# First loads on two queues and in smaller parts, constant matmuls ahead of the data, another accumulator and GpSimd for the convolution's matrices, in a kernel of two transformer blocks

## The chip, the cores and the metric

The kernel runs on one core of a Trainium2 chip. The metric is device microseconds of one execution. TensorE multiplies matrices into eight PSUM accumulators ("banks" of 128 x 512 f32 each), VectorE, ScalarE and GpSimd do elementwise work, and DMA transfers are issued from the queue of SyncE (SP) and, after the change, of ScalarE too.

## What is computed

Two blocks on 256 tokens of 1024 features, all in f32. The part that matters here is the start of the first block:

```python
def first_block(x, p, mix_pre_norm, w_in, conv_dw_w, conv_dw_b, ...):
    h = rmsnorm(x, mix_pre_norm[i])
    u = h @ w_in[i]                        # 1024 x 3072
    u_a, u_b = u[..., :512], u[..., 512:1024]
    hq, hk, hv, hg = ...                   # 512 columns each
    y_conv = conformer_conv(u_a, u_b, ...) # u_a * sigmoid(u_b), causal depthwise
                                           # convolution of width 31, layernorm, silu
    y_ret = retention_group(hq, hk, hv, hg)
    y = concatenate([y_conv, y_ret]) @ w_out[i]
    x = x + rmsnorm(y, mix_post_norm[i])
    ...                                    # FFN, gate; then the second block
```

The second block (differential attention, neighbourhood attention, two FFNs) isn't touched.

## The kernel before

Activations lie with features on the 128 partitions: eight tiles `h[k]` of 128 x 256 tokens. Every f32 matrix product is made of three products of halves: `weights` (lines 122 to 133) casts a loaded piece `raw` to a high half on ScalarE (line 129) and takes the low half on VectorE (line 130); `split_scaled` (lines 150 to 152) does the same for x, scaled by a column of `vec`; `mm3` (lines 163 to 170) issues high by high, high by low, low by high. Loaded pieces share four buffers (`raw`), the halves five each (`hi`, `lo`), activations a ring of 16 (`x`).

`w_in` comes in blocks of 256 output columns. Block 0 is computed piece by piece while x arrives (lines 313 to 327): four pieces of 512 columns, each followed by two tiles of x, all issued from SP, behind `vec` (all constant columns, among them the norm's weights and the convolution's taps, line 101). `in_products` (line 329) makes a further block from two loads of 512 KB. Its accumulator comes from the pool `pmm`, which has three; the pool `pss` has two, for the convolution and the scores, and `pst` two, for small products.

The norm's reciprocal isn't applied to x but to the products. Squares of x are summed beside the work (`Stat`, from line 196), two tiny products and a power on GpSimd (line 194) make the reciprocal `rx`, and `times_r` (line 338) multiplies a finished accumulator by it, which also frees the accumulator. Blocks 0 to 3 feed the convolution. Channel group 0 is done with 31 taps on VectorE (line 396), groups 1 to 3 as products on TensorE (line 387): 32 x 32 diagonal matrices `cw` are made from `vec` by VectorE (line 372, two instructions a group, six in all, pinned behind the last weight split by `conv_pin`), and shifted copies of the input by ScalarE and VectorE (line 381). Blocks 4 to 7 are queries and keys.

A scheduler orders each engine's instructions by the program's order and by simulated times in which they become ready, and hands out the buffers of a pool as they come free; on the chip each engine then works through its list in that order.

## Time and profile before

| | us |
|---|---|
| median of 3 runs | 1422.79 (1421.12 to 1423.82) |
| the profiled execution | 1420.28 |
| its span, first to last instruction | 1418.4 |
| TensorE busy in the span | 1376.9 (97%) |
| VectorE, ScalarE, GpSimd busy | 1060.8, 697.1, 64.8 |
| loaded from HBM | 237.10 MB |

Times in the rows below are microseconds from the start of the span; an engine's idle time before an instruction stands in square brackets with what ended it. A matmul's end is modelled, so the distance between starts tells its pace.

### The profile page before, as it was taken

Reading aid. Unit: us, or ns where it says so; the run is one execution under the profiler, and the core shown is the slowest. Engines: PE = TensorE matmul, PEld = TensorE weight load, DVE = VectorE, ACT = ScalarE, POOL = GpSimd, SP = SyncE. Lnnn points to the kernel's source line nnn. Section 1 sums busy time; section 2 is a strip of 40 time slices with the busy share of each in tenths; the row PEclk is TensorE's granted clock in tenths of the full one; section 3 lists DMA queues with packets and bytes.
Section 4 is the critical chain, followed back from the end, with each engine's and each line's share of the span. In section 5 each row is a group of like instructions: output and inputs, shape, how many; then the busy total and the mean of one; then the engine's idle time right before and its main releaser. Section 6 shows DMA issues by size and latency. Waiting matters only on the chain.

```text
span 1418.4 us, 25707 instructions
## 1 busy us (share of the span) xinstructions
PE 1376.9 (97%) x9907; PEld 1260.0 (89%) x9907; DVE 1060.8 (75%) x2174; ACT 697.1 (49%) x1314; POOL 64.8 (5%) x116
## 2 busy tenths in 40 slices
PE   7998999999998999999999999999999999999997
PEld 6898899999997898799888888888998788899997
DVE  7975889986576789977799999965765457777653
ACT  6655544454464777654422222223554446654442
POOL 0000000000000223220000000000000000000000
PEclk9999999999999999999999999999999999999999
DMA  8457598667463334324565776634632224365462
GB/s 302 133 163 267 179 316 278 214 212 228 125 205 122 105 120 125 107 87 145 167 212 194 217 236 222 207 124 128 199 127 72 80 89 136 123 196 184 146 184 92
DMA packets 77739, 239.83 MB, mean 169 GB/s; under 512 B 8752, under 2 KB 13104, under 8 KB 77488
## 3 DMA queue, kind: packets, MB, share of 16 engines
q1 hardware_dynamic: 77616, 238.18, 52.2%
q8 instruction: 78, 1.28, 0.4%
q14 instruction: 45, 0.37, 0.1%
HBM read 237.10 MB, written 1.05 MB: 168 GB/s over the span
## 4 chain that ended last, share of the span: by engine, by line
PE 79%; issue 14%; ACT 2%; DVE 2%; DMA 2%; POOL 1%; SPq 0%; POOLq 0%; DVEq 0%; ACTq 0%
PE mm L168 20%; PE mm L169 19%; PE mm L170 19%; PE mm L177 2%; PE mm L178 2%; PE mm L179 2%; PE s L757 1%; PE o L1095 1%; PE t L782 1%; PE s L169 1%; PE s L170 1%; PE s L168 1%; PE s L1055 1%; PE t L1085 1%; ACT hi L129 1%
## 5 line engine op out<-in xcount | busy, mean ns | idle before, releaser
L129 ACT CAST hi<-raw 128x1024 fp32r<-128x1024 f32 (+2 forms) x382 | 365.2, 958 | 520.0 <-PE mm L169 327.3
L130 DVE TENSOR_TENSOR lo<-raw,hi 128x1024 fp32r<-128x1024 f32 (+2 forms) x382 | 422.3, 1107 | 173.3 <-ACT hi L129 170.2
L168 PE MATMUL mm<-x,hi 128*128 128x256 f32 (+2 forms) x1584 | 491.8, 314 | 13.3 <-ACT x L151 8.0
L169 PE MATMUL mm<-x,hi 128*128 128x256 f32 (+2 forms) x1584 | 491.3, 311 | 1.6 <-DVE x L619 1.3
L170 PE MATMUL mm<-x,lo 128*128 128x256 f32 (+2 forms) x1584 | 490.8, 311 | 0.8 <-DVE lo L130 0.8
L168 PEld LDWEIGHTS mm<-x,hi 128*128 128x128 f32 x1584 | 303.0, 193 | 42.3 <-issue 14.5
L170 PEld LDWEIGHTS mm<-x,lo 128*128 128x128 f32 x1584 | 304.9, 193 | 18.4 <-issue 3.4
L169 PEld LDWEIGHTS mm<-x,hi 128*128 128x128 f32 x1584 | 304.7, 193 | 17.9 <-issue 1.7
L263 DVE SCALAR_TENSOR_TENSOR junk<-adaw,sb 128x512 f32<-128x512 f32 x320 | 219.9, 687 | 11.2 <-DMA adaw<-ada 6.6
L168 PE MATMUL mm<-o,hi 128*128 128x256 f32 (+1 forms) x340 | 100.9, 303 | 2.3 <-ACT o L147 2.1
L170 PE MATMUL mm<-o,lo 128*128 128x256 f32 (+1 forms) x340 | 101.7, 301 | 0.0
L169 PE MATMUL mm<-o,hi 128*128 128x256 f32 (+1 forms) x340 | 101.5, 300 | 0.0
L168 PE MATMUL s<-x,hi 128*128 128x258 f32 (+1 forms) x304 | 86.2, 284 | 0.0
L169 PE MATMUL s<-x,hi 128*128 128x258 f32 (+1 forms) x304 | 86.2, 284 | 0.0
L170 PE MATMUL s<-x,lo 128*128 128x258 f32 (+1 forms) x304 | 86.2, 283 | 0.0
L169 PE MATMUL mm<-q,hi 128*128 128x256 f32 (+1 forms) x265 | 80.9, 305 | 0.0
L170 PE MATMUL mm<-q,lo 128*128 128x256 f32 (+1 forms) x265 | 80.8, 305 | 0.0
L168 PE MATMUL mm<-q,hi 128*128 128x256 f32 (+1 forms) x265 | 80.8, 305 | 0.0
L168 PEld LDWEIGHTS mm<-o,hi 128*128 128x128 f32 x340 | 65.2, 195 | 5.9 <-ACT o L147 2.8
L177 PE MATMUL mm<-hi,x 128*128 128x256 f32 x240 | 70.1, 292 | 0.0
L194 POOL TENSOR_TENSOR rv<-rv,mhalf 128x2 f32<-128x2 f32 (+1 forms) x16 | 14.5, 907 | 1200.3 <-DVE rv L193 1200.3
L179 PE MATMUL mm<-hi,x 128*128 128x256 f32 x240 | 69.1, 288 | 0.0
(242 smaller groups left out, 2138.5 us busy)
## 6 DMA issues: line engine op xcount, KB each, us to landing
raw<-gu SPq DMA_DIRECT2D x88, 512.0 KB, 4.0
adaw<-ada SPq DMA_DIRECT2D x80, 512.0 KB, 4.5
raw<-wqkv SPq DMA_DIRECT2D x72, 512.0 KB, 4.1
raw<-ffn SPq DMA_DIRECT2D x44, 512.0 KB, 5.4
raw<-down SPq DMA_DIRECT2D x37, 384.0 KB, 3.2
raw<-down SPq DMA_DIRECT2D x37, 320.0 KB, 3.0
raw<-w_in SPq DMA_DIRECT2D x22, 512.0 KB, 5.3
o<-ada SPq DMA_DIRECT2D x32, 256.0 KB, 5.5
```

Of the source, the lines that this page charges most:

```text
L129: last_conv[:] = [act.copy(hi[:, :n], raw[:, :n]).ins, dve.tensor_tensor(lo[:, :n], raw[:, :n], f32(hi[:, :n]), op=ALU.subtract).ins]
L130: dve.tensor_tensor(lo[:, :n], raw[:, :n], f32(hi[:, :n]), op=ALU.subtract).ins]
L168: pe.matmul(out, wh, xh, start=first and k == 0, stop=False)
L169: pe.matmul(out, wh, xl, start=False, stop=False)
L170: last_mm[0] = pe.matmul(out, wl, xh, start=False, stop=last and k == n - 1).ins
L177: pe.matmul(out, xh[:, ts_], wh, start=k == 0, stop=False)
L178: pe.matmul(out, xh[:, ts_], wl, start=False, stop=False)
L179: pe.matmul(out, xl[:, ts_], wh, start=False, stop=k == n - 1)
L194: pool.tensor_tensor(out, out, mhalf[:, :n], op=ALU.pow)
L263: dve.scalar_tensor_tensor(out=junk, in0=raw[:, gs_], scalar=1.0, in1=sb[:, v, gs_], op0=ALU.mult, op1=ALU.mult, accum_out=acc[:, n, v, g: ...
L757: mm = pe.matmul(ps[m], a_[ms, qs], b_[ms, k0:k0 + n], start=i == 0, stop=i == 2)
L782: mm = pe.matmul(po[:, :P], pT[:, j * P:(j + 1) * P], vv, start=j == 0, stop=j == nk - 1)
```

## The change

- `vec` is loaded in two parts. Its first eight columns (the weights of the first norm) are the first issue, from ScalarE's queue; the rest is issued from SP behind the loads of block 0.
- Eight f32 products of the constant tile `ones` with itself go into an accumulator of `pst` that nobody reads.
- Block 0's pieces: the first two of 256 columns, then three of 512. x0 and x1 are issued from ScalarE's queue, the others from SP.
- Block 3's accumulator comes from `pss`.
- The matrices `cw` are made on GpSimd, without the pin.

```diff
--- before.py
+++ after.py
@@
+WAKE = 8
@@
-    nc.sync.dma_start(out=vec, in_=a["vec"])
+
+    act.dma_start(out=vec[:, :8], in_=a["vec"][:, :8])
     ident = tab[:, C_ID:C_ID + P]
     ones = const.tile([P, P], F32, name="ones")
     dve.memset(ones, 1.0)
 
     first = small.tile([P, 1], F32, tag="first", name="first", bufs=1)
+
+    wake = bank(pst, "t")
+    for _ in range(WAKE):
+        pe.matmul(wake[:, :P], ones, ones, start=True, stop=True)
     act.activation(first, ones[:, 0:1], AF.Silu)
@@
-    for g in range(4):
-        raw = load(a["w_in"][0][:, g * 512:(g + 1) * 512], 512)
-        for k in (2 * g, 2 * g + 1):
-            nc.sync.dma_start(out=h[k], in_=a["x"][:, k, :])
-        (w,) = weights(None, (512,), [raw])
-        for k in (2 * g, 2 * g + 1):
+    for ks in ((0,), (1,), (2, 3), (4, 5), (6, 7)):
+        raw = load(a["w_in"][0][:, ks[0] * T:(ks[-1] + 1) * T], len(ks) * T)
+        for k in ks:
+            (act if k < 2 else nc.sync).dma_start(out=h[k], in_=a["x"][:, k, :])
+        (w,) = weights(None, (len(ks) * T,), [raw])
+        for k in ks:
@@
-                c0 = (k % 2) * T + j * P
+                c0 = (k - ks[0]) * T + j * P
@@
+    nc.sync.dma_start(out=vec[:, 8:], in_=a["vec"][:, 8:])
+
     def in_products(i):
         w = w_blocks(a["w_in"][i])
-        ps = bank(pmm, "mm")
+
+        ps = bank(pss, "s") if i == 3 else bank(pmm, "mm")
@@
-        conv_pin = last_conv[1]
@@
-            with tc.issue_after(conv_pin):
-                for i in range(nd // 16, 2):
-                    d0 = V_DWW + c * 32 + i * 16
-                    dve.tensor_tensor(
-                        cw[i].rearrange("p (n m) -> p n m", m=32), vec[:, V_MASK:V_MASK + 32].unsqueeze(1).to_broadcast([P, 16, 32]),
-                        vec[:, d0:d0 + 16].unsqueeze(2).to_broadcast([P, 16, 32]), op=ALU.mult)
+            for i in range(nd // 16, 2):
+                d0 = V_DWW + c * 32 + i * 16
+                pool.tensor_tensor(
+                    cw[i].rearrange("p (n m) -> p n m", m=32), vec[:, V_MASK:V_MASK + 32].unsqueeze(1).to_broadcast([P, 16, 32]),
+                    vec[:, d0:d0 + 16].unsqueeze(2).to_broadcast([P, 16, 32]), op=ALU.mult)
```

## Rows read from the trace of the kernel before

**Rows 1.** The page: span, and busy time of each engine with its share.

```profile
span 1418.4 us, 25707 instructions
PE 1376.9 (97%) x9907; PEld 1260.0 (89%) x9907; DVE 1060.8 (75%) x2174; ACT 697.1 (49%) x1314; POOL 64.8 (5%) x116
```

**Rows 2.** Waits of TensorE, 0 to 62 us: total, times, longest.

```profile
PE mm L168 <- ACT x L151: 6.2, 1, 6.2
PE mm L168 <- DVE t L338: 2.4, 1, 2.4
```

**Rows 3.** Stretches: length, busy times (instructions), clock, DMA share, GB/s.

```profile
0.00:6.20 6.20, 0.00 (x0) 0.00 (x0) 1.52 (x14) 2.63 (x5) 0.19 (x4) 1.00 0.61 189
6.20:14.70 8.50, 8.17 (x49) 7.57 (x49) 6.81 (x17) 7.26 (x17) 0.00 (x0) 1.00 1.00 357
14.70:28.80 14.10, 13.34 (x109) 12.93 (x108) 12.25 (x16) 7.70 (x11) 0.70 (x1) 1.00 0.85 297
...
31.20:133.80 102.60, 102.60 (x926) 95.10 (x926) 80.37 (x148) 65.94 (x131) 2.72 (x3) 1.00 0.55 182
```

**Rows 4.** TensorE in order of time: start, duration, line, shapes, idle before.

```profile
9.48 0.41 PE L169 MATMUL mm<-x,hi 128*128 128x256 f32 x1
9.70 0.41 PE L170 MATMUL mm<-x,lo 128*128 128x256 f32 x1
...
10.12 0.29 PE L169 MATMUL mm<-x,hi 128*128 128x256 f32 x1
10.25 0.28 PE L170 MATMUL mm<-x,lo 128*128 128x256 f32 x1
...
15.95 0.39 PE L170 MATMUL mm<-x,lo 128*128 128x256 f32 x1 [0.76 <-DVE lo L130]
```

**Rows 5.** The chain that ended last, 0 to 20 us: start, duration, what.

```profile
7.56 6.00 DMA raw<-w_in
...
13.58 1.06 ACT hi L129
```

**Rows 6.** TensorE in order of time: two f32 products of the norm and the next matmul.

```profile
27.12 0.60 PE L229 MATMUL t<-tab,rv 128*128 128x128 f32 x4
27.48 0.37 PE L168 MATMUL mm<-x,hi 128*128 128x256 f32 x1
```

**Rows 7.** SP's queue in order of time: its first issue.

```profile
0.72 0.38 SPq L101 DMA_DIRECT2D vec<-vec  x1
```

**Rows 8.** ScalarE in order of time.

```profile
0.71 1.28 ACT L107 ACT_TABLE_LOAD   x1 [0.71 <-PEq L1312]
...
35.46 2.01 ACT L438 ACTIVATE sb<-sb 128x1024 f32<-128x1024 f32 x2 [0.15 <-DMA sb<-sb]
37.37 7.09 ACT L381 COPY o<-q 32x284 f32<-32x284 f32 x16
```

**Rows 9.** TensorE in order of time: the convolution's first pair and the next matmul.

```profile
40.46 0.62 PE L387 MATMUL s<-o,x 128*32 128x256 f32 x2
41.01 0.38 PE L169 MATMUL mm<-x,hi 128*128 128x256 f32 x1
```

**Rows 10.** VectorE in order of time.

```profile
24.70 1.23 DVE L130 TENSOR_TENSOR lo<-raw,hi 128x1024 fp32r<-128x1024 f32 x1 [1.04 <-ACT hi L129]
...
27.94 2.51 DVE L130 TENSOR_TENSOR lo<-raw,hi 128x1024 fp32r<-128x1024 f32 x2 [0.81 <-ACT hi L129]
30.37 1.28 DVE L338 TENSOR_TENSOR t<-mm,rstd 128x512 f32<-128x512 f32 x2
```

**Rows 11.** Line 372, all its instructions: min/median/max ns, first and last start.

```profile
L372 DVE TENSOR_TENSOR x<-vec x6: 684/686/687, 17.4 to 26.4; 128x512 f32<-128x512 f32 x6
```

**Rows 12.** GpSimd by line and shape: busy us, mean ns, idle before.

```profile
L769 POOL TENSOR_TENSOR sc<-sc 128x1 f32<-128x1 f32 x32 | 13.4, 420 | 93.0 <-ACT e L766 93.0
L194 POOL TENSOR_TENSOR rv<-rv,mhalf 128x2 f32<-128x2 f32 x14 | 12.5, 893 | 1187.0 <-DVE rv L193 1187.0
L194 POOL TENSOR_TENSOR rv<-rv,mhalf 128x4 f32<-128x4 f32 x2 | 2.0, 1008 | 13.3 <-DVE rv L193 13.3
```

## The prediction

> **What bounds the kernel now.** I read the busy times first: TensorE has 97% of the span [rows 1], so the question is where it stands still and whether that time can move to the end. The waits of TensorE over the first 62 us come second [rows 2]: 6.2 us until the first scaled x, and one stall of 2.4 us that a VectorE product by the norm's reciprocal (line 338) ends. That product frees an accumulator: the pool `pmm` has three, the blocks c = 0, 1, 2 of `in_products` fill them, and c = 3 can't start until block 0 has been read. The table by stretches [rows 3] ties these together. Until 6.2 nothing is on TensorE; until 14.7 the first block runs while the DMA engines are full (share 1.00, 357 GB/s); then blocks 1 and 2; from 31.2 to 133.8 TensorE is busy for 102.60 of 102.60 us. So whatever TensorE gains ahead of 31.2 slides through some 100 us in which it alone is the bound, provided that its inputs come earlier too. Behind 133.8 loads are paced by buffers that TensorE frees, so I let the shift go through to the end.
>
> In TensorE's order of time [rows 4], the first block's matmuls stand 0.22 us apart (9.48 to 9.70) and 0.13 us apart from 10.12 on: the lower of its two levels (1.2 GHz), after 6.2 us of nothing, and then 2.4 GHz. The last stall of this stretch ends at 15.95, when the low halves of block 1's first weights are there. The chain of work that ended last [rows 5] says why so late: the load lands at 13.56 and the cast starts at 13.58, so it is the transfer, with no slack, and not TensorE's pace in block 0.
>
> **The change part by part.**
>
> *Constant matmuls.* Eight f32 128x128 products on `ones` are queued ahead of the data. Two such products (four instructions, line 229) take 0.60 us at the upper level, or 0.36 to the start of the next matmul [rows 6], so 0.18 to 0.30 each and twice that at the lower one: 2.9 to 4.8 us for eight. They can start at about 1.1, when `ones` is set, and end at 4.0 to 5.9, where TensorE now has nothing to do [rows 2]. What they can save is at most the slow part of block 0, 6.24 to 10.12 at 0.22 in place of 0.12: about 18 matmuls by 0.1 us, 1.8 us. But block 1 waits for its load until 15.95 in any case, so the saving turns into a longer wait there. I take 0; if the first data are ready before the eight are through, they hold block 0 up by some tenths, which the same wait at block 1 covers.
>
> *First loads.* `vec` is cut: eight columns go out first on ScalarE's queue, the rest (some 0.23 MB) behind x. The first 512 columns of weights go in two halves, and x0, x1 are issued from ScalarE. An issue takes some 0.4 us of a queue [rows 7]. SP issues 13 transfers before block 1's in place of 14, so that one goes out some 0.5 us earlier; ScalarE has three issues and a table load of 1.28 us [rows 8] before its first cast, so x0 is issued at 1.2 if it comes before the table load and at 2.6 if behind it, and the first data matmul falls at 4.6 or 5.5 in place of 6.24. Block 0 ends perhaps 2 us earlier. What counts is block 1's load, though, and ahead of it lie the same bytes as now (w_in's first block, x, `vec`, `tab`). It comes earlier only as far as the DMA engines fill sooner: their share is 0.61 in the first 6.2 us [rows 3], so 2.4 us are unused, of which about 1.5 are the start before any data. Bounds 0 and 0.9 us; I take 0.6, nearer to the upper end because two queues issue and no large `vec` stands in front. The Trainium skill (DMA: Bandwidth & Descriptors, "Issuing engines are not separate DMA queues") says that issuing from several engines saves only the issuer's time, since all feed the same 16 engines; by that rule the term is nearer 0 and the whole sum 0.6 us smaller. The full share from 6.2 us on agrees with it. The fifth piece of block 0 needs the buffer of the first (four in the ring), free at about 4.4 us, when SP would come to it anyway: 0.
>
> *Fourth bank.* Block 3 goes to an accumulator of `pss`, which stands empty until the convolution's first product at 40.46 [rows 9]. The 2.40 us go if nothing else is late at 28.8: its second low half is ready at 24.70 + 1.23 = 25.9 [rows 10], so yes. Next is block 4, 48 matmuls by 0.12 behind 28.8, at 34.6, less what came before: weights at 27.94 + 2.51 = 30.5 and the accumulator of block 0 by 31.0 [rows 10], 3 us ahead. The next late thing is the convolution's first product, which would be reached at 40.46 - 3.0 = 37.5. It needs two ScalarE copies, which start at 37.37 behind the two activations on `sb`, and these started at 35.46, when a load of 1 MB had landed [rows 8]: ready at 38.2, 0.7 us late, if that load doesn't come sooner. Between 0 and 0.7 us are given back; I take 0.3.
>
> *GpSimd for the matrices.* Six VectorE products of 128x512, 686 ns each [rows 11], 4.1 us in 17 to 27 us, go to GpSimd and lose the pin behind the weight splits. TensorE doesn't wait for VectorE in that stretch (its stalls are all named above), so taking them off is worth 0 at once; it gives the low halves room, which the earlier TensorE needs. GpSimd's price for that shape isn't in the trace. Below: a product of one column, 0.42 us. Above: the power function grows from 893 to 1008 ns for two columns more, 57 ns a column, 29 us for 512 [rows 12]. A product is not a power function (0.42 us for one column against 0.89 for two), and the nearest row in shape and operation is VectorE's own 0.69; I take 1.3 us, twice that, 8 us for six. They start when the rest of `vec` lands, near 10.4. The first two are needed at 37.5, so up to 13 us each is free there; the power of the norm, if it is queued behind all six, is late for TensorE from about 3 us each. So 0, with a wait from 3 us upward. The Trainium skill (GPSIMD Engine Reference, "3.1 Elementwise") gives 2.6 cycles an element at 1.2 GHz, by which I estimate 1.1 us.
>
> *Sum.* 2.4 + 0.6 - 0.3 = 2.7 us. The profiled execution took 1420.28 us (span 1418.4 [rows 1] and 1.9 around it), which would become 1417.6. The median of the runs is 1422.79, 2.5 above it; the same shift gives 1420.1.
>
> **The rivals.**
>
> *The two engines shut each other out.* From 10.4 us on VectorE works nearly without a break on instructions that read two operands from SBUF (lines 130, 152, 212): 12.25 of 14.1 us in the third stretch [rows 3]. If a GpSimd product holds VectorE's second operand off while it runs, six by 1.3 us alternate with VectorE's, and those that fall ahead of block 1's low halves at 15.95 cost TensorE their full length, since that wait has no slack. Three to six of them: 4 to 8 us, against the 2.7 gained: 1.3 to 5 us slower, 1424 to 1428; I put it at 1426.2. It is slower than before once VectorE is held up by more than 2.7 us there. For it: VectorE is full just there, and today's six products were pinned behind the splits. Against it: nothing in this trace, as GpSimd only ever reads single columns beside VectorE. The Trainium skill (SBUF — State Buffer, "Who interferes with whom") states it as a rule: a VectorE instruction with two SBUF inputs and a GpSimd instruction that reads SBUF take turns on one port for a whole instruction. No run here shows it yet.
>
> *The bank does not serve.* The two accumulators of `pss` belong to the convolution; if block 3 gets one only behind the convolution of c = 1, it runs late, block 4 takes its place and waits for the same line 338. Then 0.6 us remain: 1422.2. The program traces two convolution tiles ahead of block 3; that the tiles are handed out in the order in which work becomes ready speaks against it.
>
> *The order of the convolution's products.* A lone pair of them holds the next long matmul up by 41.01 - 40.46 = 0.55 us [rows 9], where the same two in a long run take some 0.1, so every break costs about 0.5 us; their 192 instructions stand in six runs now, of which the first stands there. Other ready times mean another order: two breaks fewer or four more, -1 to +2 us. With four more, 1422.1.
>
> *The start is worth more.* If the transfers really come 2 us earlier (block 1's load at 11.5) and the copies too, 2.4 + 2 to 2.4 + 3: 1417.9. The DMA share of 1.00 from 6.2 us on is against it.
>
> **How the numbers follow.** About 0.2%, 2.8 us, is what a measurement of this kernel can tell from no change. The forecast (1420.1, alone 1418 to 1421.5) has 0.50, just at that border: 0.29 faster, 0.21 the same. The start that is worth more 0.17, all faster. The bank that doesn't serve and the broken order 0.15, the same. The shut-out 0.18: 0.04 the same, 0.14 slower. Together faster 0.46, same 0.40, slower 0.14; I move 0.02 from the same to slower, for a power function that comes late. The range must leave out no more than 2 in 10: 1416.8 to 1426.2, which takes in most of the better start and half of the shut-out.
>
> **What would show it.** Right: products on `ones` at 1 to 4.5 us; data matmuls 0.12 us apart from the first; the wait for line 338 gone from TensorE's list; block 1 starting between 15.0 and 15.9; no VectorE products of line 372's kind; the stretch of unbroken TensorE starting near 15 and ending near 131. Wrong: block 1 at 18 or later, with lines 130 or 212 longer than 1.23 and 0.42 us while GpSimd is busy (shut out); a wait before block 3 or the same wait before block 4 (bank); block 1 before 14 (the start); more runs of line 387's kind. If TensorE is 2.7 us ahead at 60 us and not at the end, the shift was given back behind 133.8, which I don't expect.

## The result, and the profile after

The changed kernel takes 1431.84 us (median; 1421.97 for the kernel before), a ratio of 1.0061 [1.0047, 1.0075], or 8.7 us slower by the ratio. One of its six executions took 2709.18 us; the ratio leaves it out, and the other five have a median of 1431.40. 2.7 us faster was forecast, and the time lies outside the range. The profiled execution of the kernel before (1420.28 us) is shorter than its median, so distances read between rows can be some 2 us larger than those by the ratios. The page of the profiled execution (1430.13 us), the lines that answer to [rows 1]: busy time and share of each engine.

```profile
span 1428.3 us, 25747 instructions
PE 1389.3 (97%) x9923; PEld 1268.2 (89%) x9923; DVE 1063.4 (74%) x2169; ACT 696.9 (49%) x1315; POOL 73.9 (5%) x122
```

TensorE's busy time grew by 12.4 us, more than the span (9.9), of which the constant matmuls are 3.8. So the loss is not one more wait; TensorE works longer at the same products. The waits of TensorE over the first 62 us say the same: the two of [rows 2], 6.2 and 2.4 us, are gone, and what took their place is smaller.

```profile
PE mm L175 <- DVE x L158: 2.5, 1, 2.5
PE mm L174 <- ACT x L157: 1.6, 2, 1.4
PE t L112 <- DVE ones L106: 1.0, 1, 1.0
PE mm L176 <- DVE lo L136: 0.5, 1, 0.5
```

Where the time went is seen by counting TensorE's instructions by stretch (length, busy time and count, granted clock, DMA share, GB/s). First the kernel before, in which 8 of the 117 in the first stretch belong to the norm, then the one after, with 16 of 77 on the constant:

```profile
0.00:24.00 24.00, 16.72 (x117) 1.00 0.82 276
24.00:40.46 16.46, 14.06 (x117) 1.00 0.77 289
```

```profile
0.00:24.00 24.00, 18.23 (x77) 0.86 0.67 216
24.00:40.80 16.80, 16.80 (x142) 1.00 0.92 328
```

109 data products (weights by x) are through by 24 us before, 61 after. The 48 that are missing are 5.7 us at 0.12 us each, and the norm's eight products (0.8 us) are still to come: the changed kernel is 6.5 us behind. From 24 us to the convolution the changed kernel stands still for nothing and wins back the 2.4 us. The convolution costs 2.3 us more (15.1 against 12.8 us on TensorE, from the starts of its runs and of what follows them), and the data products between its runs some 1.0 us more. That makes 7.4 us. The last product ahead of the next norm starts at 133.57 us before and at 141.38 after, 7.8 us later. By that norm's power on GpSimd, at 139.46 and 146.35, it is 6.9, because the norm's two groups of four products took 0.98 and 0.99 us before and 0.58 each after. The shift stays near 7.0 up to 430 us. It becomes 8.1 where TensorE waits 3.6 in place of 2.4 us for ScalarE at the attention's start, 9.5 between 582 and 597 us, and it ends at 10.0. With the step from 8.1 to 9.5 goes TensorE's level: the granted clock of two stretches that answer to each other, before and after, is 0.80 and 0.50.

```profile
585.00:590.00 5.00, 4.42 (x26) 0.80 0.48 170
```

```profile
592.00:597.00 5.00, 5.00 (x22) 0.50 0.64 211
```

The start in TensorE's order of time, after (start, duration; the idle time before it in brackets):

```profile
1.03 3.79 PE L112 MATMUL t<-ones 128*128 128x128 f32 x16 [1.03 <-DVE ones L106]
5.04 0.58 PE L174 MATMUL mm<-x,hi 128*128 128x256 f32 x1 [0.22 <-ACT x L157]
6.58 0.41 PE L176 MATMUL mm<-x,lo 128*128 128x256 f32 x1
8.38 0.58 PE L174 MATMUL mm<-x,hi 128*128 128x256 f32 x1 [1.40 <-ACT x L157]
...
13.34 0.41 PE L174 MATMUL mm<-x,hi 128*128 128x256 f32 x1
13.55 0.39 PE L175 MATMUL mm<-x,hi 128*128 128x256 f32 x1
...
17.35 0.58 PE L175 MATMUL mm<-x,hi 128*128 128x256 f32 x1 [2.46 <-DVE x L158]
...
21.53 0.58 PE L176 MATMUL mm<-x,lo 128*128 128x256 f32 x1 [0.46 <-DVE lo L136]
```

The first data product comes 1.2 us earlier than before, starves after six, and the starts stay 0.21 us apart until 13.55 (before: until 10.12, [rows 4]). It stands again for 2.46 us, and the next products are at the lower level once more. The first low half of block 1 comes at 21.53 in place of 15.95. Why x was late: ScalarE, then SyncE.

```profile
3.64 0.40 ACT L135 CAST hi<-raw 128x256 fp32r<-128x256 f32 x1 [0.99 <-DMA raw<-w_in]
3.65 0.33 ACTq L324 DMA_DIRECT2D h<-x  x1
7.83 1.31 ACT L157 ACTIVATE x<-h,vec 128x256 fp32r<-128x256 f32 x3 [2.16 <-DMA h<-x]
```

```profile
5.62 2.53 SPq L324 DMA_DIRECT2D h<-x  x2
...
9.20 3.80 SPq L124 DMA_DIRECT2D raw<-w_in  x4
```

x1's issue stands behind ScalarE's first cast, which waits for its weights, so x1 is scaled at 7.83. SyncE holds its last two loads of x until another load of x has landed (a wait of 1.8 us), and the loads of block 1 go out at 9.20 (before: the one that counts at 7.56, [rows 5]).

### The profile page after: what moved, and what is told of

It is laid out like the page before. It is cut to its first block, busy times and chain, and to the rows that moved or that the text cites. A ratio compares the mean times of both kernels' runs of the same rounds, so it can differ in the third digit from the quotient of the medians.

```text
span 1428.3 us, 25747 instructions
## 1 busy us (share of the span) xinstructions
PE 1389.3 (97%) x9923; PEld 1268.2 (89%) x9923; DVE 1063.4 (74%) x2169; ACT 696.9 (49%) x1315; POOL 73.9 (5%) x122
## 4 chain that ended last, share of the span: by engine, by line
PE 79%; issue 14%; DVE 3%; ACT 2%; DMA 1%; POOL 1%; SPq 0%; DVEq 0%; POOLq 0%; ACTq 0%
PE mm L174 19%; PE mm L176 19%; PE mm L175 19%; PE mm L183 2%; PE mm L184 2%; PE mm L185 2%; PE s L764 1%; PE o L1102 1%; PE t L789 1%; PE s L175 1%; PE s L176 1%; PE s L174 1%; PE s L1062 1%; PE s L394 1%; PE t L1092 1%
## 5 line engine op out<-in xcount | busy, mean ns | idle before, releaser
L135 ACT CAST hi<-raw 128x1024 fp32r<-128x1024 f32 (+3 forms) x383 | 365.1, 956 | 520.4 <-PE mm L175 318.7
L136 DVE TENSOR_TENSOR lo<-raw,hi 128x1024 fp32r<-128x1024 f32 (+3 forms) x383 | 423.9, 1108 | 176.4 <-ACT hi L135 172.2
L176 PE MATMUL mm<-o,lo 128*128 128x256 f32 (+1 forms) x340 | 101.8, 301 | 0.0
L174 PE MATMUL s<-x,hi 128*128 128x258 f32 (+1 forms) x320 | 90.8, 284 | 0.0
L176 PE MATMUL s<-x,lo 128*128 128x258 f32 (+1 forms) x320 | 90.8, 284 | 0.0
L175 PE MATMUL s<-x,hi 128*128 128x258 f32 (+1 forms) x320 | 90.7, 284 | 0.0
```

The source lines that it names most:

```text
L135: last_conv[:] = [act.copy(hi[:, :n], raw[:, :n]).ins, dve.tensor_tensor(lo[:, :n], raw[:, :n], f32(hi[:, :n]), op=ALU.subtract).ins]
L136: dve.tensor_tensor(lo[:, :n], raw[:, :n], f32(hi[:, :n]), op=ALU.subtract).ins]
L174: pe.matmul(out, wh, xh, start=first and k == 0, stop=False)
L175: pe.matmul(out, wh, xl, start=False, stop=False)
L176: last_mm[0] = pe.matmul(out, wl, xh, start=False, stop=last and k == n - 1).ins
```

## The experiments

Three theories stood at the start: GpSimd's products hold VectorE off and so TensorE (the prediction's rival); the first loads come late, through x1's issue and the wait on SyncE; or the order of the work changes, the convolution's products first of all. Each part of the change was made alone in the kernel before, and nearly each was taken out of the changed kernel. All ratios are against runs of the kernel before on the same chip; "norm" is the start of VectorE's four products that normalise the convolution (93.40 before, 100.68 in the changed kernel), "p wait" TensorE's wait for the cast of the tile p near 110 us, "last product" the start of TensorE's last product ahead of the norm near 140 us, and "wait behind" TensorE's wait for that norm's sums. "Data products" are those through by 24 us. These five columns come from one profiled execution of each kernel.

| kernel | us | ratio [95%] | data products | norm | p wait | last product | wait behind |
|---|---|---|---|---|---|---|---|
| before | 1422.0 to 1423.9 | | 109 | 93.4 | none | 133.6 | 3.4 |
| changed | 1431.84 | 1.0061 [1.0047, 1.0075] | 61 | 100.7 | none | 141.4 | 3.3 |
| e2: matrices on GpSimd alone | 1421.23 | 0.9991 [0.9980, 1.0003] | 98 | 98.7 | 0.2 | 136.3 | 1.0 |
| e4: fourth bank alone | 1425.12 | 1.0017 [1.0006, 1.0028] | 110 | 99.9 | 0.2 | 137.4 | 1.1 |
| e11: constant matmuls alone | 1423.67 | 1.0013 [1.0001, 1.0025] | 101 | 94.1 | none | 134.6 | 3.0 |
| e10: five pieces alone | 1422.49 | 1.0002 [0.9990, 1.0014] | 90 | 95.4 | none | 135.5 | 3.2 |
| e9: split of vec alone | 1428.99 | 1.0046 [1.0031, 1.0060] | 75 | 103.0 | 3.7 | 142.9 | 1.0 |
| e5: all of the first loads | 1428.18 | 1.0034 [1.0022, 1.0045] | 84 | 104.7 | 3.4 | 144.3 | 1.0 |
| e6: the same, x0 and x1 on SyncE | 1426.85 | 1.0028 [1.0015, 1.0041] | 103 | 100.2 | 3.4 | 140.2 | 1.0 |
| e12: five pieces, vec whole on ScalarE | 1425.05 | 1.0016 [1.0002, 1.0030] | 103 | 95.7 | none | 136.1 | 4.4 |
| e1: changed, matrices on VectorE | 1431.87 | 1.0056 [1.0041, 1.0072] | 81 | 103.0 | 4.5 | 144.5 | 1.0 |
| e3: changed, GpSimd only writes | 1429.48 | 1.0044 [1.0029, 1.0059] | 71 | 98.8 | none | 139.1 | 4.0 |
| e7: changed, x0 and x1 early | 1430.55 | 1.0059 [1.0040, 1.0078] | 68 | 99.9 | none | 140.9 | 4.0 |
| e8: changed, three banks | 1429.60 | 1.0050 [1.0032, 1.0068] | 56 | 100.8 | none | 141.4 | 3.5 |
| e14: changed, vec whole | 1429.43 | 1.0050 [1.0031, 1.0069] | 89 | 101.3 | 4.1 | 141.9 | 1.0 |
| e13: five pieces and GpSimd | 1428.79 | 1.0037 [1.0024, 1.0049] | 94 | 101.1 | 3.9 | 142.1 | 1.0 |
| e17: e13, p off SyncE | 1426.03 | 1.0020 [1.0008, 1.0033] | 93 | 101.8 | 1.7 | 138.7 | 1.0 |
| e15: bank of its own | 1425.53 | 1.0013 [1.0002, 1.0025] | 97 | 98.7 | 3.6 | 138.7 | 1.0 |
| e16: e15 and GpSimd | 1420.90 | 0.9982 [0.9972, 0.9992] | 97 | 96.8 | none | 134.2 | 1.5 |
| e18: changed, mended | 1425.89 | 1.0015 [1.0005, 1.0025] | 89 | 100.3 | 1.7 | 137.2 | 1.0 |

### GpSimd's products (e1, e2, e3)

The first theory was the rival of the prediction: the two engines shut each other out. It has a clear mark in the changed kernel: while GpSimd is busy, VectorE's instructions of 0.69 and 0.42 us take 1.56 and 1.29.

```profile
10.99 7.23 POOL L379 TENSOR_TENSOR x<-vec 128x512 f32<-128x512 f32 x6 [10.56 <-DMA vec<-vec]
```

```profile
11.07 1.56 DVE L136 TENSOR_TENSOR lo<-raw,hi 128x512 fp32r<-128x512 f32 x1
12.56 1.29 DVE L218 TENSOR_TENSOR acc<-acc,sq 128x256 f32<-128x256 f32 x1
```

To tell it apart the matrices went back to VectorE in the changed kernel (e1), to GpSimd in the kernel before (e2), and in e3 GpSimd only sets those tiles to zero, which leaves the convolution of three channel groups out of the result.

```diff
# e1, in the changed kernel          # e2, in the kernel before: the other way round
-            for i in range(nd // 16, 2):
+        conv_pin = last_conv[1]
+            with tc.issue_after(conv_pin): for i in range(nd // 16, 2):
-                pool.tensor_tensor(cw[i] ...)
+                dve.tensor_tensor(cw[i] ...)
# e3, in the changed kernel
-                pool.tensor_tensor(cw[i] ...)
+                pool.memset(cw[i], 0.0)
```

> The changed kernel with the six convolution matrices back on VectorE, pinned as before; all else as changed. Theory 1 (GpSimd's products hold VectorE's two-operand instructions off): no low half or sum longer than 1.23 and 0.42 us in 10 to 20 us, block 1's low halves there at 15 to 16.5 us instead of 21.5, time 1424 to 1427. Theory 2 (the loss is in the first loads: x1 issued from ScalarE behind a cast, and TensorE at its lower level): block 1 still starts at 19 us or later and the time stays within 2 us of 1431.8.

> The kernel before with one change: the six matrices on GpSimd, no pin. Theory 1: VectorE's instructions lengthen by about 1.2 us each while GpSimd is busy; vec lands at 3.5 us here, so the six products meet block 0's halves at 5 to 14 us, block 0 ends 3 to 6 us later, and the time is 1424 to 1428. Theory 2: 1421 to 1423.

> The changed kernel, but GpSimd fills the six matrices with zeros instead of multiplying, so the convolution's products on three of four channel groups are left out of the result. GpSimd still writes the same tiles but reads none. Theory 1 in the form that the operands GpSimd reads are what holds VectorE off: VectorE's instructions keep their lengths and the time is that of the run with the matrices on VectorE, 1424 to 1427. If any GpSimd work blocks VectorE: low halves up to 2 us long and 1429 to 1432. Theory 2: 1430 to 1432.

The first theory fell as the cause of the whole loss. e1 has no GpSimd product, and VectorE's instructions have their old lengths there, but the first low half of block 1 still comes at 19.39 us (before 15.95, changed 21.53), and e1 is as slow as the changed kernel. What it wins at the start it loses near 110 us, where TensorE waits 4.5 us for p.

```profile
19.39 0.39 PE L176 MATMUL mm<-x,lo 128*128 128x256 f32 x1 [0.76 <-DVE lo L136]
```

So GpSimd's products hold the start up by some 2.1 us (19.18 in e3), and the other 3.4 stay without them. (e3 sets its zeros by 3.6 us, ahead of the data, so it doesn't show whether writing alone holds VectorE off.) e2 has all six, at 3.50 to 10.98 us and with VectorE lengthened in the same way (two products of line 152 take 2.49 us in place of 0.88), and is no slower than before. It has little to spare, though: its last product ahead of the norm comes 2.7 us later than before, and the wait behind is 2.4 us shorter. In the changed kernel, the price in time is the difference to e3, which keeps the changed kernel's runs of the convolution: 2.4 us, with intervals that overlap. The 2.46 us wait for VectorE at 17.35 is what is seen of it.

### The fourth bank (e4, e8, e15, e16)

```diff
# e4, in the kernel before           # e8, in the changed kernel: the other way round
-        ps = bank(pmm, "mm")
+        ps = bank(pss, "s") if i == 3 else bank(pmm, "mm")
# e15, in the kernel before; e16 the same, with the matrices on GpSimd
-        ps = bank(pmm, "mm")
+        ps = bank(pso, "o") if i == 3 else bank(pmm, "mm")
```

> The kernel before with one change: block 3's accumulator from the pool of the convolution. If block 3 gets it at once: no wait of 2.4 us at 28.8, 1419 to 1420.5. If the scheduler puts block 4 first and block 3 behind the convolution: the wait for the reciprocal's product stays, now ahead of block 4, and runs of the convolution's products change from 6 to as many as 11, 0.5 us a run: 1422 to 1425.

> The changed kernel without the fourth bank: block 3's products go into the bank ring of three again. Theory B (the bank is one of the two that the convolution's groups use, so block 3 stands behind the first two groups instead of ahead of them, which cost 2.5 us when done alone): the convolution's products come in 6 runs instead of 11, block 3 stands ahead of them again, and the time is 1427.5 to 1430. If the order follows from the matrices on GpSimd or from the start instead, the time stays at 1431 to 1433.

> The kernel before with block 3 in the one bank of the fourth ring (the one that the attention's outputs use later), which is empty in this stage, instead of a bank of the convolution's ring. Block 3 keeps its place ahead of the convolution's products and PE does not wait 2.4 us for DVE's first product with rstd. If the prediction's term was right for a bank that is free, 1419 to 1421.5; if what follows (block 4's bank, DVE) takes the wait's place, 1421.5 to 1423.5.

> The same bank of its own together with the matrices on GpSimd, nothing else of the change: the version that keeps the two parts which alone did not cost. If both help, 1418 to 1420.5; if GpSimd's products only shift VectorE's work, 1419.5 to 1422; if VectorE's shut-out at the start weighs, 1422 to 1425.

TensorE in e4, in order of time: the product that waits, the convolution's first two groups, and block 3.

```profile
32.20 0.58 PE L168 MATMUL mm<-x,hi 128*128 128x256 f32 x1 [3.42 <-DVE t L338]
42.58 4.13 PE L387 MATMUL s<-o,x 128*32 128x256 f32 x70
46.96 3.64 PE L387 MATMUL s<-o,x 128*32 128x256 f32 x58
50.53 0.39 PE L168 MATMUL s<-x,hi 128*128 128x256 f32 x1
```

The ring `pss` has two banks, and both are given to the convolution's first two groups ahead of block 3. Block 3 therefore runs at 50.53, behind them, block 4 moves up, and the same wait for line 338 is 3.42 us long in place of 2.40, with 12 products at the lower level behind it (32.6 to 34.9 us, some 0.09 us more each). The changed kernel has the same place of block 3 (55.05, right behind the second group's last run). So the bank didn't free block 3; it moved it, and alone it costs 2.4 us where a gain of 2.4 was the largest term of the sum. The convolution keeps six runs in e4; up to 11 were thought possible. Without the bank (e8) the changed kernel is 1.6 us faster by the ratios, with intervals that overlap, and the convolution has 9 runs, not the 6 that were expected.

The bank of the fourth ring is empty at that time. With it the wait for line 338 is gone (e15: TensorE idle for 0.0 us from 24 to 40.2), and still e15 is not faster, and slower than both times that were expected: the normalisation comes at 98.7, and 3.6 us are spent at 107.47, on p. In e16 the same bank with the matrices on GpSimd has no such wait, and it is the only kernel here that is faster than before, by 0.18% [0.08%, 0.28%], a time that was expected if GpSimd only shifts VectorE's work. TensorE's waits in e16 from 24 to 135 us, where e2 has 2.9 us of them, are one line:

```profile
PE mm L169 <- DVE x L148: 0.5, 2, 0.3
```

So the wait of the prediction's term does go if the bank is one that nobody holds. That it is worth time isn't shown: e16 reaches the convolution 1.2 us of work ahead of the kernel before (at 39.78 us, with four data products more done), but its last product ahead of the norm starts at 134.23, 0.7 us later than before. It is ahead only behind that place, where the wait is 1.45 us in place of 3.43. Against e2 (0.9982 and 0.9991) the intervals overlap.

### The first loads (e5, e6, e7, e9, e10, e12)

```diff
# e5, in the kernel before: the whole of the change's first loads
# e6: e5 with x0, x1 on SyncE
-            (act if k < 2 else nc.sync).dma_start(out=h[k], in_=a["x"][:, k, :])
+            nc.sync.dma_start(out=h[k], in_=a["x"][:, k, :])
# e7, in the changed kernel: ahead of the loop over the pieces
+    for k in (0, 1):
+        act.dma_start(out=h[k], in_=a["x"][:, k, :])
# e9, in the kernel before
-    nc.sync.dma_start(out=vec, in_=a["vec"])
+    act.dma_start(out=vec[:, :8], in_=a["vec"][:, :8])
...
+    nc.sync.dma_start(out=vec[:, 8:], in_=a["vec"][:, 8:])    # behind block 0's loads
# e10, in the kernel before: the pieces alone; e12: e10 and vec whole from ScalarE
-    for g in range(4):
+    for ks in ((0,), (1,), (2, 3), (4, 5), (6, 7)):
```

> The kernel before with one part of the change: the first loads in five pieces, x0, x1 and the first 8 columns of vec issued from ScalarE, the rest of vec behind the pieces; matrices, bank and PE's first matmuls as before. Theory L (the start is the main loss): x1's load stands behind ScalarE's first cast and lands at about 8.8 us, SyncE's sixth load of x waits for that landing, and the loads of the second block go out near 10 instead of 7.56 us; block 1's first low half then comes at 18.5 to 20 us instead of 15.95, and the time is 1424.5 to 1428. Theory O (the order in which the planner places the convolution's products and the fourth bank costs it, the start is swallowed by the 2.4 us wait for a bank that follows): 1421.5 to 1424.

> As the run with the first loads alone, but x0 and x1 issued from SyncE, as all other loads of x. Theory L: no load of x stands behind a cast, SyncE's sixth load of x waits for nothing that is late, the second block's loads go out at 7.5 to 8.5 us, and the time is 1421 to 1424, at least 1.5 us under the run with the two loads on ScalarE. A rival, that the smaller pieces themselves or the late rest of vec cost the time, expects both runs within 1 us of each other.

> The changed kernel with one edit: ScalarE issues the loads of x0 and x1 before the loop over the pieces, so that x1's stands ahead of the first cast (issue near 2 instead of 3.65 us); all else as in the changed kernel. Theory L: x1 lands by 6.5 us, SyncE's hold of 2 to 3 us before its last loads of x is gone, and the time falls by 2 to 4 us, to 1428 to 1430. If the hold is not x1's, the time stays at 1431 to 1432.5.

> The kernel before with the split of vec alone: its first 8 columns from ScalarE, the rest from SyncE behind the four pieces of block 0; pieces, loads of x, bank and matrices as before. Theory V (what is left of the loss with x on SyncE is the order that the planner makes of a later vec: convolution's products in 8 runs instead of 6, the mean of the convolution later, and PE meets a 3.4 us wait near 109 us on the x that ScalarE writes): the same 3.4 us wait, 8 runs, and 1425 to 1427.5. A rival, that the smaller pieces cost it (more issues on SyncE, matmuls that start early and starve at the lower clock): 1421.5 to 1424.

> The kernel before with block 0's weights in five pieces instead of four, all loads from SyncE and vec whole and first, as before. Theory V: the planner's order of the convolution stays (6 runs, no wait near 109 us), the first matmul comes 0.8 to 1.3 us earlier, the last pieces 0.4 us later, and the time is 1421 to 1424, no difference beyond 0.1 %. The rival expects 1425 to 1427.5 here.

> A version meant to keep what the change's first loads give without their cost: five pieces and all of x on SyncE, vec whole but issued first from ScalarE, so that SyncE's first piece goes out 0.43 us earlier and the planner's order of the convolution stays that of before (6 runs). If the first loads are worth something, 1419.5 to 1422; if the start is swallowed by the wait for a bank that follows, 1421.5 to 1424.

Of the three parts of the first loads the split of vec is the dear one: 6.5 us alone; all three together have 4.8, with intervals that overlap. The five pieces cost nothing and give nothing. x0 and x1 on ScalarE make the start late in the way seen above, since e6 has 103 data products by 24 us and e5 84; in time it is 0.9 us of ratio, within the intervals. e7 cures that hold (SyncE's last loads of x go out at 6.15 and block 1's at 8.00) and gains nothing that can be told from its interval, where 2 to 4 us were expected. Issuing vec from ScalarE (e12) brings 103 data products where e10 has 90, but no time: 0.16% slower than before, outside both of its expectations. The Trainium skill (DMA: Bandwidth & Descriptors, "Issuing engines are not separate DMA queues") says that a second issuing engine saves issue time alone; e5, e6 and e12 agree.

e6 is the one that puzzles: its start is nearly as good as the kernel's before (the first power on GpSimd at 23.04, before 23.75), and yet it is 4 us slower, where 1421 to 1424 us were expected if the start were all. What it shares with e9, e5, e1 and e14 stands under "norm" and "p wait".

### The order behind the start, and p (e13, e14, e17)

The split makes the rest of vec late: the taps' factor 0.5 and the matrices come from it, and in the lists that the scheduler made for e5, e6, e9 and e13 the convolution's products stand in eight runs in place of six, the first of them behind 226 data products in place of 220. That the scheduler does so because it takes vec to be late in its simulated times is argued, not shown. Shown is that the order comes without the split too: e13 has vec whole and first, five pieces and GpSimd's matrices, two parts that cost nothing alone.

```diff
# e13, in the kernel before: five pieces (e10) and the matrices on GpSimd (e2)
# e14, in the changed kernel
-    act.dma_start(out=vec[:, :8], in_=a["vec"][:, :8])
+    nc.sync.dma_start(out=vec, in_=a["vec"])
-    nc.sync.dma_start(out=vec[:, 8:], in_=a["vec"][:, 8:])
# e17, in e13
-    nc.sync.dma_start(out=pt, in_=a["p"])
+    pool.dma_start(out=pt, in_=a["p"])
```

> The kernel before with five pieces (all on SyncE, vec whole and first) and the matrices on GpSimd: the planner then gives the convolution the same order as with the split of vec (8 runs instead of 6, mean of the convolution 27 products later on PE), but the start is that of before. If the order costs, the 3.4 to 3.7 us wait near 109 us comes back and the time is 1425 to 1428; if the start alone costs, 1421 to 1423.5.

> The changed kernel with vec loaded whole from SyncE ahead of all else, as before; pieces, x0 and x1 from ScalarE, matmuls on the constant, bank and GpSimd as in the changed kernel. If the split costs by the start (a second block that comes late, TensorE at the lower level), most of its 6.5 us come back: 1424.5 to 1428. If by the order, which stays one of 8 runs here, 1428.5 to 1432.

> The kernel of the run with five pieces and the matrices on GpSimd (1428.79 us), with one edit: p is loaded from GpSimd's queue instead of SyncE's, where it stands behind the context's loads that wait for the convolution's normalisation. The order of PE's work stays. If that chain is the price of the order: p's cast comes by 104.5 instead of 109.4 us, the 3.9 us wait near 110 us is gone or under 1 us, the lower level that follows it too, and the time is 1424 to 1426.5. If the price lies elsewhere (convolution's products, VectorE), 1427.5 to 1429.5.

e13 is 5.3 us slower than before and e14 gives back only 1.6 of the changed kernel's 8.7, as was expected if the order costs, and not if the start does. (The times of e4, e5, e9 and e13 lie 0.1 to 1.5 us above the ranges that were expected.) But the number of runs alone doesn't say whether TensorE waits for p: e15 has six runs and waits 3.6 us. How the order costs time is read along four engines: VectorE's normalisation, SyncE's loads of the context and of p, ScalarE's cast of p. The kernel before, then e13:

```profile
93.40 1.41 DVE L414 TENSOR_TENSOR t<-hc,t 128x256 f32<-128x256 f32 x4 [1.90 <-PE t L229]
...
93.85 1.75 SPq L463 DMA_DIRECT2D hc<-ctx  x4
...
96.40 0.38 SPq L466 DMA_DIRECT2D x<-p  x1
...
101.41 0.62 ACT L147 CAST x<-x 128x512 fp32r<-128x512 f32 x1 [2.78 <-DMA x<-p]
```

```profile
101.06 1.41 DVE L412 TENSOR_TENSOR t<-hc,t 128x256 f32<-128x256 f32 x4 [2.38 <-PE t L229]
...
101.50 1.76 SPq L461 DMA_DIRECT2D hc<-ctx  x4
...
104.07 0.37 SPq L464 DMA_DIRECT2D x<-p  x1
...
109.43 0.62 ACT L147 CAST x<-x 128x512 fp32r<-128x512 f32 x1 [2.09 <-DMA x<-p]
...
110.10 1.01 PE L168 MATMUL mm<-x,hi 128*128 128x256 f32 x3 [3.89 <-ACT x L147]
```

The context is loaded into the tiles `hc` in which the convolution's results stand, so its loads wait for the normalisation; p, which has nothing to do with it, is queued behind them on SyncE. On TensorE the convolution ends only 2.7 us later in e13 (59.9 against 57.2); on VectorE, whose list has changed too, the last tap of channel group 0 starts 5.6 us later (79.88 against 74.30). A normalisation that is 7.7 us later makes p 7.7 us later, and TensorE, which used p at most 3.6 us after it was ready before (VectorE ends p's low half at 102.8; the copy of the first product of p starts at 107.85, and the product is twelve matmuls by 0.12), runs into it and then works at the lower level (18 products until 115.1). This also says how two parts that alone cost nothing can cost 5.3 us together, though no run separates it from the new order: five pieces alone make the normalisation 2.0 us later (e10), GpSimd's matrices 5.3 (e2), both 7.7, and p's cast is 1.7, 3.6 and 8.0 us later. Each alone stays within the 3.6 us, e2 just so (a p wait of 0.2); both together don't.

e17 takes p off that queue and keeps TensorE's order:

```profile
98.74 0.75 POOL L464 DMA_DIRECT2D x<-p  x1
...
107.94 0.60 ACT L147 CAST x<-x 128x512 fp32r<-128x512 f32 x1
...
108.59 0.62 PE L168 MATMUL mm<-x,hi 128*128 128x256 f32 x3 [1.69 <-ACT x L147]
```

The cast comes only 1.5 us earlier, not 5: on ScalarE a weight cast and two activations that wait for VectorE stand in front of it (105.48 to 108.0), in the order that it has in e13 too. The wait falls to 1.69, the stretch at the lower level behind it goes, and the time to 1426.03, as the chain had it (by the ratios, 2.4 of e13's 5.3 us). In what is left (2.8 us) stand those 1.69 us and two runs more of the convolution's products (13.9 against 12.8 us).

A second place decides as well, right behind the long stretch. TensorE waits there for the sums of the next norm, and the wait differs from kernel to kernel (last column). The last product and the sums, in the kernel before and in e13:

```profile
133.57 0.28 PE L170 MATMUL mm<-x,lo 128*128 128x256 f32 x1
137.28 0.98 PE L223 MATMUL t<-ones,acc 128*128 128x1 f32 x4 [3.43 <-DVE acc L212]
```

```profile
142.06 0.28 PE L170 MATMUL mm<-x,lo 128*128 128x256 f32 x1
143.37 0.58 PE L223 MATMUL t<-ones,acc 128*128 128x1 f32 x4 [1.03 <-DVE acc L212]
```

In the kernel before, ScalarE's last squares stand behind a cast that has waited 2.36 us for a load of `ffn` and starts at 134.50; in e13 that cast starts at 139.88 and the squares wait for TensorE alone. So e13 is 8.5 us late at its last product and gets 2.4 of it back. Every kernel with a p wait has this shorter wait, and so, nearly, has e16 (1.45); the changed kernel (3.33) doesn't. This is read from the rows; no run changes that load alone.

### Constant matmuls (e11), and the changed kernel mended (e18)

```diff
# e11, in the kernel before
+    wake = bank(pst, "t")
+    for _ in range(8):
+        pe.matmul(wake[:, :P], ones, ones, start=True, stop=True)
# e18, in the changed kernel: e14's vec, e7's x0 and x1, e17's p, and
-        ps = bank(pss, "s") if i == 3 else bank(pmm, "mm")
+        ps = bank(pso, "o") if i == 3 else bank(pmm, "mm")
```

> The kernel before with the eight matmuls on the constant ahead of the data, nothing else changed. They are over at about 4.8 us and the first data come at 6.24 us. If they leave TensorE at the higher level for the data, the 14 matmuls that ran 0.21 us apart up to 10.1 us go 0.12 us apart, but the pieces then bound them: 1420.5 to 1423. If the level falls again in the gap to the data, or they move the fall to a later place, 1422 to 1425.

> The changed kernel with vec whole from SyncE, x0 and x1 from ScalarE ahead of the casts, block 3 in the empty bank of the fourth ring and p loaded from GpSimd's queue; five pieces, matmuls on the constant and GpSimd's matrices stay. If the two chains (PE's start, and VectorE's convolution with p behind it) are the whole of the loss, 1419.5 to 1423.5; if the start's gap ahead of the second block and TensorE's lower level behind it stay, 1424 to 1427.

In e11 the 16 instructions end at 4.8 us, the first data product comes at 5.93, and from 7.02 to 10.01 the products start 0.21 us apart, as before: 14 of them in either kernel. So they did not raise the level for the data. The time is 0.13% [0.01%, 0.25%] above the kernel before, while the profiled execution is as long as before's from 139 us on; what the remaining tenth is stays open. The mended kernel is 6.5 us faster than the changed one by the ratios and 2.1 us slower than the kernel before, in the range that was expected if the start stays late. It has no wait for a bank, but 1.7 us for p and 20 data products fewer by 24 us, and the two steps in the attention are there too.

## Why the prediction was wrong, point by point

Two steps failed. The first is a term of the sum: "First loads", put at 0.6 us faster, made the start late (block 1's first low half at 21.53 us in place of 15.95), and together with GpSimd's products it puts TensorE 6.5 us behind by 24 us. The second is the slide that was to carry every shift through the long stretch to the end: p was ready at most 3.6 us ahead of its use, and the wait behind the stretch is not the same in every kernel.

*What bounds the kernel.* "So whatever TensorE gains ahead of 31.2 slides through some 100 us in which it alone is the bound, provided that its inputs come earlier too." A stretch in which TensorE is busy for 102.60 of 102.60 us [rows 3] says that it never waited, not by how much each input was ahead. Behind it ran a second chain, VectorE's convolution, the loads of the context, p, with at most 3.6 us to spare. In seven of the eighteen kernels TensorE stood still for that chain (3.4 to 4.5 us). In the changed kernel both chains are late by 7 us (norm 100.7 against 93.4), so no wait for p shows; and e1 and e14, which have 81 and 89 data products by 24 us in place of 61, run into p for 4.5 and 4.1 us. That goes far to say why no single part, taken out of the changed kernel, gave more than 2.4 us back. "I let the shift go through to the end" failed as well: the wait right behind the stretch is 1.0 to 4.4 us long, and so gives back up to 2.4 us of what comes late. No kernel here has its last product ahead of that norm earlier than the kernel before.

*Constant matmuls, 0.* Their price, 3.79 us for 16 instructions, was inside the bounds of 2.9 to 4.8, and the saving 0, as said. (The slow part of block 0 has 16 products by the rows, not 18.) "Data matmuls 0.12 us apart from the first" was wrong: after the constant the lower level lasted as long as before in e11, and longer in the changed kernel, where x starved TensorE for 1.40 us.

*First loads, -0.6.* The sign was wrong. The first data product came at 5.04 us, between the 4.6 and 5.5 that were forecast, but the first low half of block 1 came 5.6 us later than before, of which some 2.1 go with GpSimd's products. The sum counted bytes and issues. It left out that x1's issue stands behind a cast on ScalarE (the table load was weighed, the cast wasn't) and that SyncE's last loads wait for x1's landing: block 1's loads went out 1.6 us later, not 0.5 earlier. And it put the late rest of vec at nothing, since the matrices had time until 37.5; e9 puts 6.5 us on that split alone, with 75 data products by 24 us and a p wait of 3.7 us. The rule of the Trainium skill (DMA: Bandwidth & Descriptors, "Issuing engines are not separate DMA queues"), by which the term would be nearer 0, was nearer than mine.

*Fourth bank, -2.4.* The rival "the bank does not serve" had the mechanism to the letter (block 3 behind the convolution of c = 1, block 4 in its place, the same wait for line 338), with a chance of 0.15 shared with another. What I set against it, that tiles are handed out as work becomes ready, did not hold: the two banks of `pss` went to the two convolution groups that the program traces ahead of block 3. Its price was too small, since I let the wait stay at 2.4 us and block 3 come late for nothing; alone the part measured +2.4 us. With a bank that is free the wait goes (e15, e16), but no run shows that this makes the kernel faster.

*GpSimd's matrices, 0.* Right as a net, and in part by luck: six products take 7.23 us, 1.2 us each (1.3 was taken), and alone they cost nothing (0.9991); by the rows that is because p had 3.6 us to spare and the wait behind the stretch got 2.4 us shorter, neither of which was in the working. The sign that was written down for the shut-out (block 1 at 18 or later, longer instructions on VectorE) was seen, at 20.27 and 1.29 us, and yet it didn't tell the rivals apart: e1, without GpSimd's products, has block 1 at 18.13. The rival's rule is borne out by VectorE's 1.56 and 1.29 us, so the Trainium skill (SBUF — State Buffer, "Who interferes with whom") agrees with the trace, but the price was too high: 4 to 8 us were taken, 2.4 is the difference to e3, and nothing is lost in e2, where the products run at 3.5 to 11 us and not at 11 to 18.

*The order of the convolution's products.* "Every break costs about 0.5 us" was right in size: 11 runs in place of 6 make 15.1 us of 12.8. The rival said two breaks fewer or four more, +2 us at most; there were five more, and with what the data products between them lose it is 3.3. The runs of the changed kernel in part:

```profile
40.80 0.62 PE L394 MATMUL s<-o,x 128*32 128x256 f32 x2
41.78 0.62 PE L394 MATMUL s<-o,x 128*32 128x256 f32 x2
42.88 3.65 PE L394 MATMUL s<-o,x 128*32 128x256 f32 x60
```

*The sum and the range.* Each of the five parts was priced on the kernel before as if the others weren't there and as if every engine's order stayed. The parts that alone measured 0 (five pieces, GpSimd) make 5.3 us together (e13). The range ended at the shut-out, 1426.2; it had no case in which several edits move the order of an engine that TensorE doesn't wait for yet.

*Left open.* What makes the scheduler change the order; the two steps in the attention, 2.5 us together (by GpSimd's powers at 429 and 633 us), which stand in the changed kernel and at 2.4 to 2.6 us in e1, e3, e4, e14, e15 and e18, but at 1.8 to 2.0 in e2, e10 and e16, at 0.8 to 1.2 in e7 to e9, e13 and e17, and between -0.3 and 0.3 in e5, e6, e11 and e12; and 2.1 us of the mended kernel.

## What to carry to other kernels

An engine that is busy without a gap hides how far ahead its inputs are: before a shift is let through a long stretch, look up, for each input that some other queue brings, when it was ready and when it was used, and look at what TensorE waits for right behind the stretch. A load stands behind whatever its queue waits for, so list what is issued ahead of it on the same queue (p behind the context, x1 behind a cast) and move the one that is free of the others. And a bank, or a tile, is free only if the ring that it comes from has one left at that point of the program; where a scheduler orders the work, compare the order of each engine with the edit and without it before adding up waits.

## What the runs showed of the hardware

While six products of 128x512 run on GpSimd, VectorE's two-operand instructions take 1.2 to 1.6 us in place of 0.4 to 0.7, three times as long in the worst row, and e2 as a whole still takes no longer. Sixteen f32 instructions on a constant, ended 1.1 us ahead of the data, left the data at 0.21 us a product for as long as without them. In e9 a wait of 1.99 us before block 1 is followed by a further 0.76 us and then by products at the lower level (granted clock 0.60 and then 0.50, TensorE's instructions in stretches of 5 us):

```profile
10.00:15.00 5.00, 3.42 (x27) 1.00 0.98 341
15.00:20.00 5.00, 3.63 (x16) 0.60 0.72 243
20.00:25.00 5.00, 5.00 (x26) 0.50 0.87 285
```

So two microseconds of idle time were followed by some nine microseconds in which a product took 0.21 us (17.25 to 26.0), while the kernel before, with waits of 0.29 and 0.76 us at the same place, kept the upper level: an early end of block 0 turned into time lost. The length of a wait alone doesn't say which comes: behind its 2.40 us at 31.20 the kernel before worked on at 0.12 us a product, and behind 2.57 us at 32.16 e12 took 0.21 us for 12 of them.
